# A layer on one core: two of four weight sums by accumulating loads, and a fourth unit with seven products

## The chip, the cores and the metric

The kernel runs on one core of a Trainium2 chip. The metric is the device time of one execution in microseconds (us). The engines are PE (matrix multiply), DVE (vector), ACT (scalar), POOL and SP; SP and ACT issue plain loads, and POOL can issue loads that add what they bring to what stands in the destination.

## The reference

One decoder layer of width 2048 on 256 rows in float32: a SwiGLU half step, two token mixers with gates, and a second SwiGLU half step, each between two RMS norms. The change touches the SwiGLU steps.

```python
def swiglu(x, w_gate, w_up, w_down):                 # 256x2048; 2048x5504 twice; 5504x2048
    return (jax.nn.silu(x @ w_gate) * (x @ w_up)) @ w_down

f1 = swiglu(rms_norm(h, ffn1_pre_norm[l]), ffn1_w_gate[l], ffn1_w_up[l], ffn1_w_down[l])
h = h + 0.5 * rms_norm(f1, ffn1_post_norm[l])
m = hybrid_token_mixer(rms_norm(h, mix_pre_norm[l]), ...)
h = h + rms_norm(m, mix_post_norm[l])
f2 = swiglu(rms_norm(h, ffn2_pre_norm[l]), ffn2_w_gate[l], ffn2_w_up[l], ffn2_w_down[l])
h = h + 0.5 * rms_norm(f2, ffn2_post_norm[l])
```

## The kernel before

A float32 product is made of three matmuls of a cheaper format (`mm3`, L141 to L144): each operand is split into a high part, rounded by ACT (L137), and a low part, the rest, by DVE (L138). `x`, transposed, lies in two row tiles (t = 0, 1) of 128 rows and 16 tiles of 128 along the width; its parts stay in SBUF. Weights come from memory in chunks of two 128-row blocks by up to 512 columns, each split after its load. `raw`, `whi` and `wlo` (chunk, high part, low part) are rings of five buffers.

`ffn` walks over the 5504 columns of gate and up in blocks of 512 (the last has 384). The first block goes through `gemm_block`; the other ten of each ffn go through `gemm_pair`, which makes gate and up of both row tiles at once, in four accumulators `c[t][i]`. It walks over eight units `u` of two weight blocks each. A plain unit takes 2 row tiles x 2 blocks x 2 matrices = 8 products. A unit named in `SUMS` takes seven by Strassen's scheme (Winograd's form): some products take sums of the four weight blocks with sums of the four blocks of `x`, and three products go straight into `c`. Four more accumulators, p1, p5, p6 and p7, gather over the units of `SUMS`, and in the last unit are added to `c` (L260 to L264 and the end of the function). `SUMS` is (2, 4, 6). The sums of `x` (`d`, `s2`, `s3`, `s4`) are made once in each ffn by `operand_sums`.

In a unit of seven products, `ra` holds the two blocks of gate and `rb` those of up. DVE makes the four weight sums with four adds (`wsum` twice, one in place in each of `rb` and `ra`, L248). Split are `ra` and `rb` as chunks, the two sums in `wsum` (into two tiles `wsumh`) and the sum of all four (into the tile `wall`).

The tiles `wsum`, `wsumh`, `wall` and the later `psum` come from a pool `rows` of four buffers of 2 x 512 columns. In `out_proj` the same pool holds eight rows of 512 for the norms, two in a tile.

The engines each run their instructions in order. A tile framework traces the loops, gives a pool's buffers out again when their last reader is done, puts semaphores in, and moves instructions of one engine past each other by its own estimates; so the built order, not the loops, tells what stands behind what. Loads of weights are all on SP's queue: a load that waits for a buffer holds up those behind it.

Of the kernel before, what the change touches and what calls it, by code (L numbers as in the profile page):

```python
# [7 lines left out]
F32 = mybir.dt.float32  # L8
F32R = mybir.dt.float32r
# [3 lines left out]
ALU = mybir.AluOpType  # L13
AX = mybir.AxisListType

P = 128
# [6 lines left out]
CB = 512  # L23
# [4 lines left out]
RW = -(-2 * (16 + CB) * 4 // LINE) * LINE // 4  # L28
STEPS = ((3, 2, 2, 2), (6, 2, 2, 2))
RING = 5  # L30
AHEAD = 3
SUMS = (2, 4, 6)
O_GQ, O_GK, O_GV, O_GO, O_CODE = 0, 512, 1024, 2048, 3072
O_HQ, O_HF, O_HI, O_HO, O_ZG, O_ZH = 3088, 4112, 5136, 6160, 7184, 9232

# [40 lines left out]
def kernel(ctx: ExitStack, tc: tile.TileContext, a: dict, out: bass.AP):  # L76
    nc = tc.nc
# [11 lines left out]
    uid, last = [0], [None]  # L89

    def nm(s):
        uid[0] += 1
        return f"{s}_{uid[0]}"
# [42 lines left out]
    def split_into(hi, lo, src):  # L136
        last[0] = nc.scalar.activation(hi, src, AF.Copy)  # L137
        nc.vector.tensor_tensor(lo, src, hi.bitcast(F32), op=ALU.subtract)  # L138
# [50 lines left out]
    def operand_sums(x, new_part, out):  # L189


        yield
        sl = [slice(2 * SUMS[0] + i, None, 2 * (SUMS[1] - SUMS[0])) for i in range(2)]
        n = len(SUMS)

        def views(s, m):
            t = row_tile(s).rearrange("p i c -> p (i c)")
            return [t[:, i * n * P:(i + 1) * n * P].rearrange("p (k c) -> p k c", c=P)
                    for i in range(m)]

        ab = []
        for t in range(NT):
            ab.append(views("ab", 2))
            for i in range(2):
                nc.vector.tensor_tensor(ab[t][i], x[0][t][:, sl[i], :].bitcast(F32),
                                        x[1][t][:, sl[i], :].bitcast(F32), op=ALU.add)
            yield
        (a11, a12), (a21, a22) = ab
        (d, s2), (s4, s3) = views("sums", 2), views("sums", 2)
# [12 lines left out]
    def gemm_pair(ws, c0, w, lhs, sums, ready):  # L222

        c = [[ps_tile(f"c{t}{i}") for i in range(2)] for t in range(NT)]
        p = {}
        begun = set()
        nu = KT // 2  # L230

        def part(name, u):
            hi, lo = sums[name]
            i = SUMS.index(u)
            return hi[:, i, :], lo[:, i, :]

        def product(ps, x, wp, key, stop=False):
            mm3(ps[:, :w], x, wp, key not in begun, stop)
            begun.add(key)

        def load(i, k0, c0=c0, w=w):
            return wload(ws[i][k0 * P:(k0 + 2) * P, c0:c0 + w].rearrange("(k p) c -> p k c", p=P), w)

        def split(i, k0, c0=c0, w=w):
            return wchunk(None, w, raw=load(i, k0, c0, w))

        def add(o, x, y, op=ALU.add):
            nc.vector.tensor_tensor(o, x, y, op=op)  # L248

        for u in range(nu):  # L250
            k0 = 2 * u
            last_sum = u == SUMS[-1]
            if u not in SUMS:
                if u or not ready:
                    ready = [split(0, k0)] + ([split(1, k0)] if u == nu - 1 else [])
                if u == nu - 1:
                    p1, p5, p6, p7 = [p[s][:, :w] for s in ("p1", "p5", "p6", "p7")]
                    t0, t1 = row_tile("psum"), row_tile("psum")
                    r00, r01, r10, r11 = [t[:, i, :w] for t in (t0, t1) for i in range(2)]
                    nc.scalar.copy(r00, p1)  # L260
# [24 lines left out]
            split_into(allp[:, 0, :], allp[:, 1, :], ra[:, 1, :])  # L285
            if not p:
                for name in ("p1", "p5", "p7", "p6"):
# [22 lines left out]
    def load_bcast(ts, name, n, after):  # L310

        if n % 2 == 0:
            pair = row_tile("row")
            ts += [pair[:, 0, :], pair[:, 1, :]]
        with tc.issue_after(after.ins):
            nc.scalar.dma_start(ts[n], a[name][:, n * CB:(n + 1) * CB].broadcast_to([P, CB]))

    def rstd(ss, n, width, tag):

# [94 lines left out]
    def out_proj(w_dram, nkt, lhs, post, scale, pre, homes, following):  # L414
# [2 lines left out]


        acc = [[None] * 4 for _ in range(NT)]
        wpost, wpre = [], []  # L420
# [13 lines left out]
        for i, (kt, hf) in enumerate(order):  # L434
            parts = load(kt, hf)
            if 6 <= i < 14:

                row, name = (wpost, post) if i < 10 else (wpre, pre)
                if name is not None:
                    load_bcast(row, name, i % 4 + 2 & 3, last[0])  # L440
# [494 lines left out]
    x, rs = new_xT(), [None, None]  # L935
# [34 lines left out]
    def first_of(w_dram, c0):  # L970
        def chunk(i):
# [55 lines left out]
```

## Time and profile before

| | |
|---|---|
| median of 3 runs | 2142.64 us (2141.93 to 2143.45) |
| the profiled execution | 2143.8 us, its span 2142.0 us |
| PE busy | 2130.2 us, 99% |
| DVE, ACT, POOL busy | 1506.8 us (70%), 1101.6 us (51%), 34.6 us (2%) |
| moved | 410.28 MB, 192 GB/s over the span |
| issued by SP as column chunks of gate and up | 512 KB each, 384 KB in the narrow blocks |

A row of the timeline has the start in us, the duration in us, the engine, the line, the operation, the tile written and those read, the shape and the count. A row of groups has line, engine, operation, tiles, shapes and count, then busy us and mean ns of one, then idle us before them with what ended it. A row of waits has engine, line, what was waited for, us in total, times, longest. A row of windows has for each stretch its length, then busy us (and instructions) of PE, of the weight loads, of DVE, ACT and POOL, then PE's clock, the share of the DMA engines and GB/s. A row of DMA issues ends with KB of each and the median us from issue to landing. Matmuls overlap in the pipeline, so what one costs is the distance between starts.

### The profile page before, as it was taken

The page shows a single profiled execution, that of the slowest core. Times are in us where ns is not written, and L with a number is a line of the kernel's source. Part 1 is how long each engine was busy: PE and PEld are TensorE (multiplying, and loading weights), DVE is VectorE, ACT ScalarE, POOL GpSimd, SP SyncE. Part 2 cuts the span into 40 slices and gives each one's busy share as a digit, 9 for nine tenths or more (in the row PEclk, how much of TensorE's full clock was granted, in tenths as well). Part 3 has the DMA queues.
Part 4 walks back from the last instruction along what each step waited for, and adds up shares of the span by engine and source line. Part 5 has one row for each costly group of instructions (what it writes and reads, how often), then busy time and mean ns, then how long its engine had stood idle before and what let it go on. Part 6 is the DMA issues. An engine that isn't in the chain of part 4 may idle for free.

```text
span 2142.0 us, 27066 instructions
## 1 busy us (share of the span) xinstructions
PE 2130.2 (99%) x10024; PEld 1781.7 (83%) x10024; DVE 1506.8 (70%) x1821; ACT 1101.6 (51%) x1375; POOL 34.6 (2%) x87
## 2 busy tenths in 40 slices
PE   9999999999999999999999999999999999999998
PEld 7888888898888888888888888888888888898887
DVE  6889899885455754657575556577889998975455
ACT  7555565554445564444434444465555655554443
POOL 0000000000000100000000000010000000000000
PEclk9999999999999999999999999999999999999999
DMA  7666656667567456555556676755666666576663
GB/s 258 185 198 202 207 179 207 197 201 238 192 194 236 138 177 188 166 158 144 158 160 175 198 207 189 227 195 170 201 201 194 197 197 209 163 247 195 191 194 128
DMA packets 189366, 410.28 MB, mean 192 GB/s; under 512 B 13697, under 2 KB 22305, under 8 KB 189234
## 3 DMA queue, kind: packets, MB, share of 16 engines
q1 hardware_dynamic: 183440, 399.69, 60.8%
q10 hardware_dynamic: 5794, 8.87, 1.3%
q8 instruction: 78, 1.28, 0.2%
q14 instruction: 54, 0.44, 0.1%
HBM read 406.41 MB, written 2.10 MB: 191 GB/s over the span
## 4 chain that ended last, share of the span: by engine, by line
PE 98%; DMA 1%; DVE 1%; ACT 0%; issue 0%; DVEq 0%; POOLq 0%; POOL 0%; ACTq 0%
PE mm L142 10%; PE mm L144 10%; PE mm L143 10%; PE c L143 10%; PE c L142 10%; PE c L144 10%; PE acc L142 9%; PE acc L143 9%; PE acc L144 9%; PE p L144 2%; PE p L143 2%; PE p L142 2%; PE ps L328 2%; PE ps L700 1%; DMA raw<-in_ffn_w_up_dram 0%; PE ps L750 0%
## 5 line engine op out<-in xcount | busy, mean ns | idle before, releaser
L138 DVE TENSOR_TENSOR wlo<-raw,whi 128x1024 fp32r<-128x1024 f32 (+3 forms) x740 | 892.8, 1211 | 524.0 <-ACT whi L137 509.7
L137 ACT ACTIVATE whi<-raw 128x1024 fp32r<-128x1024 f32 (+3 forms) x740 | 777.4, 1051 | 891.9 <-PE mm L143 321.2
L142 PE MATMUL c<-whi,xhi 128*128 128x512 f32 (+1 forms) x860 | 333.0, 387 | 0.0
L144 PE MATMUL c<-wlo,xhi 128*128 128x512 f32 (+1 forms) x860 | 330.1, 384 | 0.0
L143 PE MATMUL c<-whi,xlo 128*128 128x512 f32 (+1 forms) x860 | 330.0, 384 | 0.0
L142 PE MATMUL mm<-whi,xhi 128*128 128x512 f32 (+1 forms) x840 | 326.4, 389 | 1.3 <-ACT xhi L387 1.2
L143 PE MATMUL mm<-whi,xlo 128*128 128x512 f32 (+1 forms) x840 | 321.0, 383 | 0.0
L144 PE MATMUL mm<-wlo,xhi 128*128 128x512 f32 (+1 forms) x840 | 321.0, 383 | 0.0
L142 PE MATMUL acc<-whi,hkhi 128*128 128x512 f32 x640 | 249.2, 389 | 0.0
L144 PE MATMUL acc<-wlo,hkhi 128*128 128x512 f32 x640 | 249.0, 389 | 0.0
L143 PE MATMUL acc<-whi,hklo 128*128 128x512 f32 x640 | 249.0, 389 | 0.0
L144 PEld LDWEIGHTS c<-wlo,xhi 128*128 128x128 f32 x860 | 161.4, 188 | 30.1
L143 PEld LDWEIGHTS c<-whi,xlo 128*128 128x128 f32 x860 | 161.5, 188 | 29.8
L142 PEld LDWEIGHTS c<-whi,xhi 128*128 128x128 f32 x860 | 161.5, 188 | 29.1
L142 PEld LDWEIGHTS mm<-whi,xhi 128*128 128x128 f32 x840 | 158.2, 188 | 31.9 <-ACT xhi L387 2.5
L144 PEld LDWEIGHTS mm<-wlo,xhi 128*128 128x128 f32 x840 | 158.0, 188 | 30.5
L143 PEld LDWEIGHTS mm<-whi,xlo 128*128 128x128 f32 x840 | 158.1, 188 | 29.5 <-issue 0.2
L144 PEld LDWEIGHTS acc<-wlo,hkhi 128*128 128x128 f32 x640 | 120.1, 188 | 25.1
L142 PEld LDWEIGHTS acc<-whi,hkhi 128*128 128x128 f32 x640 | 120.2, 188 | 24.8
L143 PEld LDWEIGHTS acc<-whi,hklo 128*128 128x128 f32 x640 | 120.2, 188 | 24.6
L248 DVE TENSOR_TENSOR wsum<-raw 128x512 f32<-128x512 f32 (+1 forms) x120 | 81.0, 675 | 16.0 <-DMA raw<-in_ffn_w_up_dram 15.0
L138 DVE TENSOR_TENSOR wsumh<-wsum,wsumh 128x1024 fp32r<-128x1024 f32 (+1 forms) x60 | 71.5, 1192 | 0.0
(246 smaller groups left out, 2350.9 us busy)
## 6 DMA issues: line engine op xcount, KB each, us to landing
raw<-in_ffn_w_down_dram SPq DMA_DIRECT2D x172, 512.0 KB, 4.6
raw<-in_w_in_dram SPq DMA_DIRECT2D x168, 512.0 KB, 3.8
raw<-in_ffn_w_up_dram SPq DMA_DIRECT2D x160, 512.0 KB, 3.8
raw<-in_ffn_w_gate_dram SPq DMA_DIRECT2D x159, 512.0 KB, 4.6
raw<-in_w_out_dram SPq DMA_DIRECT2D x32, 512.0 KB, 4.6
raw<-in_w_branch_gla_dram SPq DMA_DIRECT2D x16, 512.0 KB, 3.8
raw<-in_w_branch_hgrn_dram SPq DMA_DIRECT2D x16, 512.0 KB, 4.2
raw<-in_ffn_w_gate_dram SPq DMA_DIRECT2D x16, 384.0 KB, 4.0
```

The costliest lines, as they stand in the source:

```text
L137: last[0] = nc.scalar.activation(hi, src, AF.Copy)
L138: nc.vector.tensor_tensor(lo, src, hi.bitcast(F32), op=ALU.subtract)
L142: nc.tensor.matmul(ps, lhsT=xhi, rhs=whi, start=start, stop=False)
L143: nc.tensor.matmul(ps, lhsT=xlo, rhs=whi, start=False, stop=False)
L144: nc.tensor.matmul(ps, lhsT=xhi, rhs=wlo, start=False, stop=stop)
L248: nc.vector.tensor_tensor(o, x, y, op=op)
L328: nc.tensor.transpose(dst_ps[:, i * P:(i + 1) * P], src[:, i * P:(i + 1) * P], ident)
L700: nc.tensor.matmul(ps[:, i * 64:(i + 1) * 64], lhsT=kT[:, sl], rhs=halves(qT[:, sl])[1], start=True, stop=True)
```

## The change

`SUMS` becomes (1, 3, 4, 6): four units of each block have seven products, and two of them stand next to each other. The blocks of a unit are loaded one by one. `ra` now holds gate's first block and up's second; `rb` holds a sum and gate's second. The two sums of two blocks are made by loads: SP loads up's first block into both halves of `wsum`, and POOL issues for each half a load that adds gate's first or up's second block. DVE makes the two sums of three and four blocks with two adds. `wsum` has three sums side by side and is split into `hi` and `lo` as one, so `wall` is gone. The order of the products changes with the operands. The `rows` pool has three buffers of 3 x 512 columns in place of four of 2 x 512; `psum`, the sums of `x` and the norm rows are laid out for three to a tile, and the last two adds of `psum` become one of twice the width. Other lines are moved in number only.

```diff
-SUMS = (2, 4, 6)
+SUMS = (1, 3, 4, 6)
...
-    rows = ctx.enter_context(tc.tile_pool(name="rows", bufs=4))
+    rows = ctx.enter_context(tc.tile_pool(name="rows", bufs=3))
...
+        def block(i, kt):
+            return ws[i][kt * P:(kt + 1) * P, c0:c0 + w]
...
                     nc.scalar.copy(r00, p1)
-                    add(r01, r00, p6)
-                    add(r10, r01, p7)
-                    add(r01, r01, p5)
-                    add(r11, r10, p5)
+                    add(ru, r00, p6)
+                    add(r10, ru, p7)
+                    add(t1[:, 0:2, :w], t0[:, 1:3, :w],
+                        p5.unsqueeze(1).broadcast_to([P, 2, w]))
...
-            (ra, _), (rb, _) = load(0, k0), load(1, k0)
+            ra, rb = [ring.tile([P, RW], F32, tag="raw", name=nm("raw"))[:, :2 * w]
+                      .rearrange("p (i c) -> p i c", i=2) for _ in range(2)]
+            wsum, hi, lo = [row_tile(n, d)[:, :, :w] for n, d in
+                            (("wsum", F32), ("wsumh", F32R), ("wsuml", F32R))]
+
+            nc.sync.dma_start(ra[:, 0, :], block(0, k0))
+            nc.sync.dma_start(ra[:, 1, :], block(1, k0 + 1))
+            for i in range(2):
+                nc.sync.dma_start(wsum[:, i, :], block(1, k0))
+                nc.gpsimd.dma_start(wsum[:, i, :], block(i, k0 + i), accum_op=ALU.add)
+            nc.sync.dma_start(rb[:, 1, :], block(0, k0 + 1))
             first = wchunk(None, w, raw=(ra, False))
-
-            wsum = row_tile("wsum")[:, :, :w]
-            add(wsum[:, 0, :], rb[:, 1, :], rb[:, 0, :])
-            add(rb[:, 0, :], rb[:, 0, :], ra[:, 0, :])
-            add(wsum[:, 1, :], rb[:, 0, :], rb[:, 1, :])
+            add(rb[:, 0, :], wsum[:, 0, :], ra[:, 1, :])
+            add(wsum[:, 2, :], rb[:, 0, :], rb[:, 1, :])
             second = wchunk(None, w, raw=(rb, False))
-            hi, lo = [row_tile("wsumh", F32R)[:, :, :w] for _ in range(2)]
-            add(ra[:, 1, :], ra[:, 1, :], wsum[:, 1, :])
             split_into(hi, lo, wsum)
-            allp = row_tile("wall", F32R)[:, :, :w]
-            split_into(allp[:, 0, :], allp[:, 1, :], ra[:, 1, :])
+            third = [(hi[:, i, :], lo[:, i, :]) for i in range(3)]
...
             product(p["p1"], lhs(0, k0), first[0], "p1", last_sum)
-            product(c[0][0], lhs(0, k0 + 1), first[1], (0, 0))
-            product(c[0][1], part("s4", u), second[1], (0, 1))
+            product(c[0][1], part("s4", u), first[1], (0, 1))
+            product(c[0][0], lhs(0, k0 + 1), second[1], (0, 0))
             side.pump()
-            product(p["p5"], part("d", u), second[0], "p5", last_sum)
-            product(p["p7"], part("s3", u), (hi[:, 0, :], lo[:, 0, :]), "p7", last_sum)
-            product(p["p6"], part("s2", u), (hi[:, 1, :], lo[:, 1, :]), "p6", last_sum)
-            product(c[1][0], lhs(1, k0 + 1), (allp[:, 0, :], allp[:, 1, :]), (1, 0))
+            product(p["p6"], part("s2", u), second[0], "p6", last_sum)
+            product(p["p5"], part("d", u), third[0], "p5", last_sum)
+            product(p["p7"], part("s3", u), third[1], "p7", last_sum)
+            product(c[1][0], lhs(1, k0 + 1), third[2], (1, 0))
...
     def row_tile(s, dt=F32):
-        return rows.tile([P, 2, CB], dt, tag="row", name=nm(s))
+        return rows.tile([P, 3, CB], dt, tag="row", name=nm(s))
```

What the build makes of it on SP and DVE stands in the prediction, at the places where it is used.

More of the change, by code (lines that the diff above doesn't have):

```diff
@@ L192, in operand_sums, with view @@
         yield
-        sl = [slice(2 * SUMS[0] + i, None, 2 * (SUMS[1] - SUMS[0])) for i in range(2)]
         n = len(SUMS)
[L196 to L199, printed above, removed]
+        groups = [(slice(2 * u0, 2 * u1 + 1, 2 * (u1 - u0)), slice(g, g + 2))
+                  for g, (u0, u1) in zip(range(0, n, 2), zip(SUMS[::2], SUMS[1::2]))]
+        free = []
+        def view():
+            if not free:
+                t = row_tile("sums")
+                free.extend(t[:, i, :n * P].rearrange("p (k c) -> p k c", c=P) for i in range(3))
+            return free.pop(0)
         ab = []
         for t in range(NT):
-            ab.append(views("ab", 2))
             for i in range(2):
[L205 to L209, printed above, removed]
+                ab.append(view())
+                for k, g in groups:
+                    k = slice(k.start + i, k.stop + i, k.step)
+                    nc.vector.tensor_tensor(ab[-1][:, g, :], x[0][t][:, k, :].bitcast(F32),
+                                            x[1][t][:, k, :].bitcast(F32), op=ALU.add)
+                yield
+        a11, a12, a21, a22 = ab
+        d, s2, s3, s4 = [view() for _ in range(4)]
         nc.vector.tensor_tensor(d, a22, a21, op=ALU.subtract)
@@ L258, in gemm_pair @@
                     t0, t1 = row_tile("psum"), row_tile("psum")
-                    r00, r01, r10, r11 = [t[:, i, :w] for t in (t0, t1) for i in range(2)]
+                    r00, ru, r10 = [t0[:, i, :w] for i in range(3)]
+                    r01, r11 = [t1[:, i, :w] for i in range(2)]
                     nc.scalar.copy(r00, p1)
-                    add(r01, r00, p6)
-                    add(r10, r01, p7)
-                    add(r01, r01, p5)
-                    add(r11, r10, p5)
+                    add(ru, r00, p6)
+                    add(r10, ru, p7)
+                    add(t1[:, 0:2, :w], t0[:, 1:3, :w],
+                        p5.unsqueeze(1).broadcast_to([P, 2, w]))
                 for i in range(2):
@@ L280, in gemm_pair @@
+            add(wsum[:, 2, :], rb[:, 0, :], rb[:, 1, :])
             second = wchunk(None, w, raw=(rb, False))
-            hi, lo = [row_tile("wsumh", F32R)[:, :, :w] for _ in range(2)]
-            add(ra[:, 1, :], ra[:, 1, :], wsum[:, 1, :])
             split_into(hi, lo, wsum)
-            allp = row_tile("wall", F32R)[:, :, :w]
-            split_into(allp[:, 0, :], allp[:, 1, :], ra[:, 1, :])
+            third = [(hi[:, i, :], lo[:, i, :]) for i in range(3)]
             if not p:
-                for name in ("p1", "p5", "p7", "p6"):
+                for name in ("p1", "p6", "p5", "p7"):
@@ L307, in row_tile, with load_bcast @@
     def row_tile(s, dt=F32):
-        return rows.tile([P, 2, CB], dt, tag="row", name=nm(s))
[L310 to L314, printed above, removed]
+        return rows.tile([P, 3, CB], dt, tag="row", name=nm(s))
+    def load_bcast(t, name, n, after):
         with tc.issue_after(after.ins):
-            nc.scalar.dma_start(ts[n], a[name][:, n * CB:(n + 1) * CB].broadcast_to([P, CB]))
+            nc.scalar.dma_start(t, a[name][:, n * CB:(n + 1) * CB].broadcast_to([P, CB]))
     def rstd(ss, n, width, tag):
@@ L419, in out_proj @@
         acc = [[None] * 4 for _ in range(NT)]
-        wpost, wpre = [], []
+        wpost, wpre, free = [], [], []
         nxt, rs, ready = ([None] * NT, [None] * NT, [0] * NT), [None, None], []
@@ L439, in out_proj @@
                 if name is not None:
-                    load_bcast(row, name, i % 4 + 2 & 3, last[0])
+                    if not free:
+                        t3 = row_tile("row")
+                        free += [t3[:, j, :] for j in range(3)]
+                    row.append(free.pop(0))
+                    load_bcast(row[-1], name, i % 4 + 2 & 3, last[0])
             for t in range(NT):
```

## The prediction

> **What bounds the kernel now.** I read the head of the page first, then the chain of waits, then what the matrix engine waited for, then one block of columns by its timeline.
>
> ```profile
> span 2142.0 us, 27066 instructions
> PE 2130.2 (99%) x10024; PEld 1781.7 (83%) x10024; DVE 1506.8 (70%) x1821; ACT 1101.6 (51%) x1375; POOL 34.6 (2%) x87
> ...
> PE 98%; DMA 1%; DVE 1%; ACT 0%; issue 0%; DVEq 0%; POOLq 0%; POOL 0%; ACTq 0%
> ...
> PE ps L963 <- POOL idle L960: 1.3, 1, 1.3
> PE mm L142 <- ACT xhi L387: 1.2, 1, 1.2
> PE ps L965 <- DMA wrow<-in_ffn_pre_norm_dram: 0.7, 1, 0.7
> PE ps L328 <- DVE hn L522: 0.7, 2, 0.4
> ...
> SPq L119 <- DVE wlo L138: 1611.1, 662, 16.7
> ```
>
> PE is busy for 99% of the span, and its four groups of waits come to 3.9 us in the whole run. So every matmul taken away is worth its start-to-start time, as long as nothing new makes PE wait. That second half is what this forecast turns on. The stage that changes is the block of columns in `gemm_pair`:
>
> ```profile
> 204.57 0.39 PE L142 MATMUL c<-whi,xhi 128*128 128x512 f32 x1
> ...
> 206.84 0.39 PE L143 MATMUL c<-whi,xlo 128*128 128x512 f32 x1
> ...
> 218.48 0.57 ACT L260 COPY psum<-p 128x512 f32<-128x512 f32 x1
> 430.96 0.59 ACT L260 COPY psum<-p 128x512 f32<-128x512 f32 x1
> 466.15 0.46 ACT L260 COPY psum<-p 128x384 f32<-128x384 f32 x1
> ...
> 176.50:218.50 42.00, 42.00 (x191) 34.84 (x190) 37.76 (x44) 24.05 (x28) 0.00 (x0) 1.00 0.64 200
> ```
>
> The first two rows are ten matmuls apart: 2.27 / 10 = 0.227 us each, so 0.681 us for a product of three. The copy of p1 stands once in each block: (430.96 - 218.48) / 5 = 42.5 us for a block of 512 columns, and 466.15 - 430.96 = 35.2 us for the narrow one of 384. In the window PE is busy for all 42.0 us, DVE for 37.8, ACT for 24.1, and the DMA engines for a share of 0.64 at 200 GB/s. There are 18 wide and 2 narrow blocks (ten in each ffn).
>
> **What the change takes away.** A fourth unit has seven products instead of eight: 0.681 us per wide block, by width 0.51 per narrow one, 18 x 0.681 + 2 x 0.51 = 13.3 us. On DVE a seven-product unit had four adds, three splits of 1024 and one of 512; it has two adds, two splits of 1024 and one of 1536:
>
> ```profile
> L138 DVE TENSOR_TENSOR wlo<-raw,whi 128x1024 fp32r<-128x1024 f32 x698 | 851.4, 1223 | 508.1 <-ACT whi L137 493.7 <-PE ps L328 8.9 <-PE ps L684 1.5
> L137 ACT ACTIVATE whi<-raw 128x1024 fp32r<-128x1024 f32 x698 | 740.4, 1061 | 859.7 <-PE mm L143 318.3 <-PE acc L143 248.0 <-PE c L143 232.8
> L248 DVE TENSOR_TENSOR raw<-raw,wsum 128x512 f32<-128x512 f32 x54 | 37.3, 690 | 1.3
> L138 DVE TENSOR_TENSOR wall<-raw,wall 128x512 fp32r<-128x512 f32 x54 | 37.1, 687 | 0.3 <-ACT wall L137 0.3
> L137 ACT ACTIVATE wall<-raw 128x512 fp32r<-128x512 f32 x54 | 33.3, 617 | 0.0
> L138 DVE TENSOR_TENSOR wlo<-raw,whi 128x768 fp32r<-128x768 f32 x32 | 30.2, 954 | 5.0 <-ACT whi L137 5.0
> L137 ACT ACTIVATE whi<-raw 128x768 fp32r<-128x768 f32 x32 | 27.0, 847 | 26.6 <-PE c L143 21.0 <-ACT wall L137 1.6 <-PE p L143 1.5
> L248 DVE TENSOR_TENSOR raw<-raw,wsum 128x384 f32<-128x384 f32 x6 | 3.3, 556 | 0.1
> L137 ACT ACTIVATE wall<-raw 128x384 fp32r<-128x384 f32 x6 | 3.1, 517 | 0.7 <-DVE raw L248 0.7
> ```
>
> By length, 1536 elements cost DVE 1.22 + (1.22 - 0.69) = 1.75 us and ACT 1.06 + (1.06 - 0.62) = 1.50. DVE's unit falls from 4 x 0.69 + 3 x 1.22 + 0.69 = 7.1 us to 2 x 0.69 + 2 x 1.22 + 1.75 = 5.6; the block as a whole gets about a microsecond lighter, in spite of the fourth unit. DVE was not waited for, so that is worth nothing. Loads grow from 32 column blocks of 256 KB to 44. At the window's share a copy of all 44 would take 0.64 x 42 x 44/32 = 37 us of DMA time, and 44 us if each of the eight accumulating loads counts twice; both stay under the period found below, so bandwidth is not the bound. SP issues 28 loads in place of 16; at 0.37 us (rows below) that is 4.4 us more on a queue that waited 1611 us of the span for raw buffers.
>
> **What the change adds: a loop through one buffer.** The `rows` pool has three buffers and a seven-product unit takes all three: `wsum`, its high part, its low part. `wsum` of a unit is loaded into the buffer which the unit before gives back, and that happens when DVE has split it (of the first unit of a block: when PE has read the last low part of the block before). The build shows it, SP before and now, then DVE now (row names carry the tile's number; in brackets the semaphores that a row waits for):
>
> ```order
> L119 DMA raw_1560<-in_ffn_w_gate_dram 128x2x512
> L119 DMA raw_1562<-in_ffn_w_up_dram 128x2x512
> L119 DMA raw_1605<-in_ffn_w_gate_dram 128x2x512
> L119 DMA raw_1611<-in_ffn_w_up_dram 128x2x512
> L119 DMA raw_1648<-in_ffn_w_gate_dram 128x2x512
> ```
>
> ```order
> L119 DMA raw_1807<-in_ffn_w_up_dram 128x2x512 [waits DMAHW7_49,DMAHW5_49,DVE_49]
> L291 DMA wsum_1742<-in_ffn_w_up_dram 128x512 [waits DMASW7_49,DMASW6_49,PE_49]
> L291 DMA wsum_1742<-in_ffn_w_up_dram 128x512
> ...
> L291 DMA wsum_1827<-in_ffn_w_up_dram 128x512 [waits DMASW1_49,DMAHW5_49,DMASW0_49,DVE_49]
> L291 DMA wsum_1827<-in_ffn_w_up_dram 128x512 [waits DMAHW6_49]
> L293 DMA raw_1871<-in_ffn_w_gate_dram 128x512 [waits DMAHW7_49,DVE_49]
> L119 DMA raw_1915<-in_ffn_w_gate_dram 128x2x512 [waits DMAHW0_49,DVE_49]
> ```
>
> The base of unit 1 (`wsum_1742`) waits for PE, that of unit 3 (`wsum_1827`) for DVE. Behind it on SP stand the other loads of the coming units, which wait too.
>
> ```order
> L257 TENSOR_TENSOR raw_1871<-wsum_1872,raw_1870 128x512
> L257 TENSOR_TENSOR wsum_1872<-raw_1871 128x512
> L138 TENSOR_TENSOR wlo_1889<-raw_1871,whi_1888 128x1024
> L138 TENSOR_TENSOR wsuml_1874<-wsum_1872,wsumh_1873 128x1536
> L138 TENSOR_TENSOR wlo_1918<-raw_1915,whi_1917 128x1024
> ```
>
> That is unit 4: add, add, split of the second chunk, split of the sums, then the next unit's. The add needs the accumulated sum; every later DVE row stands behind it, and ACT's split of the second chunk, on which PE's third product waits, needs the add. So from one unit's `wsum` to the next runs a chain in which nothing overlaps: base load, accumulating load, add, ACT's second split, ACT's split of the sums, DVE's split of the sums, next base load. Its loads are priced by these rows:
>
> ```profile
> raw<-in_ffn_w_up_dram SPq DMA_DIRECT2D x160, 512.0 KB, 3.8
> raw<-in_ffn_w_up_dram SPq DMA_DIRECT2D x16, 384.0 KB, 3.5
> bg<-in_b_branch_gates_dram ACTq DMA_DIRECT2D x8, 256.0 KB, 4.1
> row<-in_ffn_post_norm_dram ACTq DMA_DIRECT2D x8, 256.0 KB, 6.0
> out_dram<-h SPq DMA_DIRECT2D x4, 256.0 KB, 2.1
> ...
> 201.42 0.37 SPq L119 DMA_DIRECT2D raw<-in_ffn_w_up_dram  x1
> ...
> 201.91 1.22 DVE L138 TENSOR_TENSOR wlo<-raw,whi 128x1024 fp32r<-128x1024 f32 x1
> 203.04 1.22 DVE L138 TENSOR_TENSOR wsumh<-wsum,wsumh 128x1024 fp32r<-128x1024 f32 x1
> ```
>
> A base of 256 KB lands after 3.2 us (0.3 less per 128 KB). No row shows an accumulating load, nor any load issued from POOL. Its bounds are the quickest and the slowest 256 KB rows, 2.1 (a store) and 6.0 (rows spread over all partitions); less than the store I leave out, since the accumulating load also reads what it adds to and can't be a gain. I take 4.1, the 256 KB load in 2 KB pieces issued from another queue than SP: it is the nearest in size, piece and issue. Then with L for it, and 0.2 for the handoffs (an estimate: the DVE rows show 0.09 of overlap on one engine, so ACT's first split counts 0.96):
>
> 3.2 + L + 0.69 + 0.96 + 1.50 + 1.75 + 0.2 = 8.3 + L = **12.4 us a unit**.
>
> The step from unit 6 to the next block's unit 1 is longer. Its base stands on SP behind the load of unit 2's up chunk, which needs the raw buffer that DVE frees by the split of the coming unit 0. In DVE's order that comes after two splits and an add: 1.13 + 1.13 + 0.60 + 1.22 (start to start, as in the rows just quoted), and 0.4 to issue: 4.5 us. It then lies behind two 512 KB loads, so lands as they do, 3.8: 0.6 more. A block takes 4 x 12.4 + 4.5 + 0.6 = **54.7 us** against PE's own 42.5 - 0.7 = 41.8. So PE waits some 13 us a block: by the distance of the units in PE's work (15 products from 1 to 3, 7 from 3 to 4, 15 from 4 to 6) 2 to 3 us before units 3 and 6, and 12.4 - 4.8 = 7.6 from unit 3 to 4.
>
> The narrow block by its rows (768 for the second chunk, 768 and the step from 384 for the sums, 192 KB a load): 3.05 + 3.95 + 0.55 + 0.75 + 1.19 + 1.35 + 0.2 = 11.0 a unit, 4 x 11.0 + 4.1 = 48.1 against 35.2.
>
> Sum: 18 x (54.7 - 42.5) + 2 x (48.1 - 35.2) = 220 + 26 = +246 us; the saved product is in it. From the profiled execution's 2143.8 us (1.8 around its span, 1.2 above the median) that makes 2390, about **2389** on the median's scale. The rest costs nothing: the longer sums of x (fp32 256 columns eight times for 384 four times) lie beside the first up block, the wider `psum` tiles replace four adds by three, and the eight rows of the norms are the same loads.
>
> [...]
>
> **The rivals.**
>
> *The loop is hidden, so the saved products count: faster, 2130.* For it speaks that PE's order moves the low parts' matmuls back, and that SP ran up to five raw buffers ahead. It needs 4 x (8.3 + L) + 5.1 below 41.8, so L below 0.9 us; the quickest 256 KB row is 2.1. Chance 0.05. A loop that just reaches the old period (L about 1.0) would be no change: 0.03.
>
> *Accumulating loads land like plain ones, 3.2 or less.* The unit is 11.5, the block 51.1, 18 x 8.6 + 2 x 9 = +173: 2316. At 2.1 it would be +85 or so, 2230. Chance of L between 2.1 and 3.2: 0.14.
>
> *The accumulating load is held up at its issue.* POOL must prepare it while DVE is at work for 37.8 of 42 us. If it has to wait out one DVE instruction of up to 1.75 us in each unit, a block takes 7 us more: 18 x 7 + 2 x 5 = 136 on top, 2525; with an L of its own of 6.0 as well the time passes 2600. The page has POOL at 2% with nothing like it, so nothing speaks against it either. Chance of more than 6.0 in all: 0.08. [...]
>
> **How the numbers follow.** The forecast (the loop with L from 3.2 to 6.0) has 0.70: 2316 to 2143.8 + 18 x 19.8 + 2 x 20 = 2540. The range takes part of the quicker landings and ends at the slowest row: 2270 to 2540, leaving out the hidden loop, the quickest landings and the held-up issue, 2 in 10 together. What this kernel can tell from no change is 0.2%, 4 us. Slower: 0.70 + 0.14 + 0.08 = 0.92; same 0.03; faster 0.05.
>
> **What would show it.** The copy of p1 about 54.7 us apart; PE idle some 13 us a block, most of it before the third product of unit 4, put down to ACT's `whi`, ACT's to DVE's `raw`, DVE's to the load of `wsum`; bases of `wsum` on SP 12 to 13 us apart within a block; DVE busy less than 70% of the span. The landing time of the accumulating load is the number that can prove me wrong: below 1 us the loop is hidden, above 6 the time is beyond my range. If PE shows no waits in the blocks, the buffer is not what I read it to be.

## The result, and the profile after

| | before | after |
|---|---|---|
| median of 4 runs | 2143.05 us (2141.93 to 2146.14) | 2534.55 us (2532.79 to 2538.48) |
| ratio, 95% interval | | 1.183 (1.181 to 1.184) |
| span of the profiled execution | 2142.0 us | 2531.0 us |

The change costs 391 us. The head of the page of after, then the largest group of what PE waited for (total us, times, longest us):

```profile
span 2531.0 us, 27551 instructions
PE 2257.7 (89%) x9964; PEld 1823.9 (72%) x9964; DVE 1492.2 (59%) x1689; ACT 1101.7 (44%) x1335; POOL 176.2 (7%) x247
...
PE c L142 <- ACT whi L137: 213.5, 75, 7.4
```

PE, which hardly waited before, now waits for ACT's high parts of weights in front of a product into `c`. No engine is full: DVE fell from 70% to 59% of a longer span. So the time isn't in the work of an engine but in a chain of waits. Its length is read from the copies of p1, one in a block, and from the windows row of the block between two of them (its columns as in the section on the profile before):

```profile
291.35 0.59 ACT L270 COPY psum<-p 128x512 f32<-128x512 f32 x1
354.45 0.59 ACT L270 COPY psum<-p 128x512 f32<-128x512 f32 x1
...
291.40:354.50 63.10, 49.06 (x194) 37.42 (x193) 37.12 (x38) 24.28 (x26) 7.11 (x8) 0.91 0.71 183
```

This block takes 63.1 us, 20.6 more than the 42.5 of before. By the same copies the wide blocks of the run take 62.3 on average (60.2 to 63.1) and the narrow ones 54.0; 18 x 19.8 + 2 x 18.8 = 394 us is the whole loss. The DMA engines are at a share of 0.71, so bandwidth is not full either. The groups of loads by size (their last number is the median us from issue to landing) show what an accumulating load takes, the last two rows, beside a plain one of the same size:

```profile
raw<-in_ffn_w_gate_dram SPq DMA_DIRECT2D x146, 256.0 KB, 2.8
wsum<-in_ffn_w_up_dram SPq DMA_DIRECT2D x144, 256.0 KB, 3.2
...
wsum<-in_ffn_w_gate_dram POOLq DMA_DIRECT2D x72, 256.0 KB, 4.6
wsum<-in_ffn_w_up_dram POOLq DMA_DIRECT2D x72, 256.0 KB, 5.9
```

One unit (the third with sums in this block) by the timelines of SP, POOL, DVE, ACT and PE; in brackets stands how long the engine was idle before and what ended it:

```profile
325.56 0.80 SPq L291 DMA_DIRECT2D wsum<-in_ffn_w_up_dram  x2
...
329.86 0.88 POOL L292 DMA_DIRECT2D wsum<-in_ffn_w_gate_dram  x1 [13.45 <-DMA wsum<-in_ffn_w_up_dram]
330.40 1.23 POOL L292 DMA_DIRECT2D wsum<-in_ffn_w_up_dram  x1
...
334.31 0.69 DVE L257 TENSOR_TENSOR raw<-wsum,raw 128x512 f32<-128x512 f32 x1 [7.64 <-DMA wsum<-in_ffn_w_gate_dram]
335.04 0.69 DVE L257 TENSOR_TENSOR wsum<-raw 128x512 f32<-128x512 f32 x1
336.26 1.22 DVE L138 TENSOR_TENSOR wlo<-raw,whi 128x1024 fp32r<-128x1024 f32 x1 [0.53 <-ACT whi L137]
338.00 1.76 DVE L138 TENSOR_TENSOR wsuml<-wsum,wsumh 128x1536 fp32r<-128x1536 f32 x1 [0.52 <-ACT wsumh L137]
...
335.17 1.06 ACT L137 ACTIVATE whi<-raw 128x1024 fp32r<-128x1024 f32 x1 [10.48 <-DVE raw L257]
336.49 1.49 ACT L137 ACTIVATE wsumh<-wsum 128x1536 fp32r<-128x1536 f32 x1 [0.26 <-DMA wsum<-in_ffn_w_up_dram]
...
336.28 0.79 PE L142 MATMUL c<-whi,xhi 128*128 128x512 f32 x1 [7.43 <-ACT whi L137]
...
339.79 0.80 SPq L291 DMA_DIRECT2D wsum<-in_ffn_w_up_dram  x2
```

Followed from the top: base at 325.56; it lands after 3.7 us in this unit; POOL issues 0.6 later, at 329.86; the accumulated sum is there after 4.45; DVE adds; ACT splits the chunk, for which PE has stood 7.43 us, then the sums, held 0.26 by the second accumulating load; DVE splits the sums until 339.76; and the next base goes out 0.03 later. That is the loop, 14.2 us long, with no slack in it; the bases of units 3, 4 and 6 go out 0.03 us after a split of the sums in all blocks of this run. How long one load took to land stands in the view of its tile, cut to its issue; for the base of this unit:

```profile
DMA to landing us min/median/max: 3.7/3.7/3.7
```

### The profile page after: what moved, and what is told of

It reads as the page before. It is cut to its first block, busy times and chain, and to the rows that moved or that the text cites. A ratio compares the mean times of both kernels' runs of the same rounds, so it can differ in the third digit from the quotient of the medians.

```text
span 2531.0 us, 27551 instructions
## 1 busy us (share of the span) xinstructions
PE 2257.7 (89%) x9964; PEld 1823.9 (72%) x9964; DVE 1492.2 (59%) x1689; ACT 1101.7 (44%) x1335; POOL 176.2 (7%) x247
## 3 DMA queue, kind: packets, MB, share of 16 engines
q0 software_dynamic: 23040, 40.90, 10.7%
## 5 line engine op out<-in xcount | busy, mean ns | idle before, releaser
L137 ACT ACTIVATE whi<-raw 128x1024 fp32r<-128x1024 f32 (+3 forms) x740 | 760.0, 1045 | 1203.3 <-DVE raw L257 531.1
L142 PE MATMUL c<-whi,xhi 128*128 128x512 f32 (+1 forms) x720 | 296.1, 411 | 213.5 <-ACT whi L137 213.5
L142 PEld LDWEIGHTS c<-whi,xhi 128*128 128x128 f32 x720 | 139.5, 194 | 267.8 <-ACT whi L137 244.6
L144 PE MATMUL c<-wlo,xhi 128*128 128x512 f32 (+1 forms) x720 | 293.1, 407 | 18.3 <-DVE wlo L138 17.4
L257 DVE TENSOR_TENSOR raw<-wsum,raw 128x512 f32<-128x512 f32 (+1 forms) x80 | 54.3, 679 | 431.9 <-DMA wsum<-in_ffn_w_gate_dram 428.1
L143 PE MATMUL c<-whi,xlo 128*128 128x512 f32 (+1 forms) x720 | 283.7, 394 | 0.0
L144 PEld LDWEIGHTS c<-wlo,xhi 128*128 128x128 f32 x720 | 140.1, 195 | 69.1 <-DVE wlo L138 44.0
L143 PEld LDWEIGHTS c<-whi,xlo 128*128 128x128 f32 x720 | 139.7, 194 | 22.7
L138 DVE TENSOR_TENSOR wsuml<-wsum,wsumh 128x1536 fp32r<-128x1536 f32 (+1 forms) x80 | 137.5, 1719 | 28.9 <-ACT wsumh L137 27.1
L292 POOL DMA_DIRECT2D wsum<-in_ffn_w_gate_dram x80 | 69.8, 873 | 1109.1 <-DMA wsum<-in_ffn_w_up_dram 555.4
```

The source lines that it names most:

```text
L142: nc.tensor.matmul(ps, lhsT=xhi, rhs=whi, start=start, stop=False)
L143: nc.tensor.matmul(ps, lhsT=xlo, rhs=whi, start=False, stop=False)
L144: nc.tensor.matmul(ps, lhsT=xhi, rhs=wlo, start=False, stop=stop)
L292: nc.gpsimd.dma_start(wsum[:, i, :], block(i, k0 + i), accum_op=ALU.add)
```

## The experiments

Four theories were set against each other. **1**: the chain through the one free `rows` buffer, whatever its links are; **1b**: a second chain behind it, through the raw buffers on SP's queue; **2**: the adding in the load is what is dear; **3**: the fourth unit, beside the third, is the cause without any load. All times are medians of 4 runs or more beside runs of before on the same chip (2143.0 to 2143.8 us).

| run | time us | ratio to before, 95% interval |
|---|---|---|
| four buffers in common | 2467.41 | 1.151 (1.149 to 1.153) |
| two buffers of its own for `wsum` | 2333.54 | 1.089 (1.087 to 1.090) |
| four sums by DVE, no accumulating load | 2190.69 | 1.022 (1.020 to 1.024) |
| POOL loads without adding | 2427.65 | 1.132 (1.130 to 1.134) |
| no second load at all | 2182.12 | 1.018 (1.017 to 1.020) |
| accumulating loads, three units | 2311.52 | 1.079 (1.077 to 1.080) |
| four sums by DVE, three units | 2142.42 | 1.000 (0.999 to 1.001) |
| own buffers, loads ahead, three units | 2210.38 | 1.031 (1.029 to 1.032) |
| one of the four sums by POOL, four units | 2162.55 | 1.009 (1.007 to 1.010) |
| the same, units 1, 2, 4, 6 | 2162.17 | 1.009 (1.007 to 1.010) |
| own buffers, POOL loads without adding | 2262.09 | 1.057 (1.054 to 1.060) |

### A fourth buffer

```diff
-    rows = ctx.enter_context(tc.tile_pool(name="rows", bufs=3))
+    rows = ctx.enter_context(tc.tile_pool(name="rows", bufs=4))
...
-                u = work.tile([P, CB], F32, tag="tmp", name=nm("u"), bufs=3)
+                if not free:
+                    t3 = row_tile("u")
+                    free.extend(t3[:, j, :] for j in range(3))
+                u = free.pop(0)
...
```

> The pool `rows` gets a fourth buffer, paid for by the three temporary rows, which move into it; the loads and the sums stay. Four units of 14.2 us and one step of 4.9 more make the block of 62 us now.
> The loop through the single buffer alone (theory 1): `wsum` no longer takes the buffer that the last split of sums frees, so a base no longer waits for that split, and PE goes back to its own 41.8 us a block: about 2130 us.
> A second loop behind it (theory 1b): a base stands on SP behind raw loads that need the buffer which DVE's split of the second chunk gives back. That split ends at 337.5 us in the unit in which the split of the sums ends at 339.8, so a unit is about 2 us shorter and the block 8: 2535 - 18 x 8 - 2 x 7 = about 2375, at most 2470.
> That accumulating costs in itself (theory 2), or that the fourth unit stands beside the third (theory 3): no change, 2535.

2467 us: 67 less, at the upper edge of what 1b allowed, far from the 2130 of theory 1 alone. SP, DVE and ACT of this run, around one base:

```profile
309.87 0.34 SPq L288 DMA_DIRECT2D raw<-in_ffn_w_gate_dram  x1
310.38 0.81 SPq L291 DMA_DIRECT2D wsum<-in_ffn_w_up_dram  x2
...
321.14 0.38 SPq L119 DMA_DIRECT2D raw<-in_ffn_w_gate_dram  x1
321.69 0.82 SPq L291 DMA_DIRECT2D wsum<-in_ffn_w_up_dram  x2
...
308.62 1.22 DVE L138 TENSOR_TENSOR wlo<-raw,whi 128x1024 fp32r<-128x1024 f32 x1 [0.53 <-ACT whi L137]
310.25 1.76 DVE L138 TENSOR_TENSOR wsuml<-wsum,wsumh 128x1536 fp32r<-128x1536 f32 x1 [0.40 <-ACT wsumh L137]
...
319.89 1.23 DVE L138 TENSOR_TENSOR wlo<-raw,whi 128x1024 fp32r<-128x1024 f32 x1 [0.48 <-ACT whi L137]
```

The base no longer waits for the split of the sums (310.38, while that split runs from 310.25; no base of this run goes out at the end of such a split). But it stands right behind a raw load that goes out when the split of the second chunk ends: 308.62 + 1.22 = 309.84 and 309.87, 319.89 + 1.23 = 321.12 and 321.14. So there are two loops through the same add, and the buffer only removed the longer one. The step between these two bases is 11.3 us, against 14.2 in the unit shown above; the block (59.3 us) gains less, since other steps grew.

### Two buffers of its own

```diff
-    rows = ctx.enter_context(tc.tile_pool(name="rows", bufs=3))
+    rows = ctx.enter_context(tc.tile_pool(name="rows", bufs=2))
...
     def row_tile(s, dt=F32):
-        return rows.tile([P, 3, CB], dt, tag="row", name=nm(s))
+        tag = "row"
+        if s in ("row", "u", "sums", "wrow", "idle"):
+            turn[0] += 1
+            tag = ("row", "wsum")[turn[0] % 2]
+        elif s == "wsum":
+            tag = "wsum"
+        return rows.tile([P, 3, CB], dt, tag=tag, name=nm(s))
...
```

> As much memory as with a fourth buffer, but `wsum` has two buffers of its own, and the high part, the low part and `psum` share the other two. A base now has to wait only for the split of the sums in the unit before the last.
> Theory 1: the loop now spans two units, so PE's waits fall by more than half: 2130 (all gone) to 2300.
> Theory 1b (the base stands behind raw loads on SP): 2375 to 2470, as with four buffers in common.
> Theories 2 and 3: 2535.

2334 us, with the memory of the run before: half of the loss is gone, but the time misses both ranges and lies between them. What PE waits for has changed. The largest group of its waits, then SP, DVE, ACT and PE in one block:

```profile
PE p L144 <- DVE wsuml L138: 138.4, 20, 8.9
...
286.30 0.80 SPq L291 DMA_DIRECT2D wsum<-in_ffn_w_up_dram  x2
...
301.16 0.82 SPq L291 DMA_DIRECT2D wsum<-in_ffn_w_up_dram  x2
...
284.52 1.75 DVE L138 TENSOR_TENSOR wsuml<-wsum,wsumh 128x1536 fp32r<-128x1536 f32 x1
...
297.04 0.69 DVE L257 TENSOR_TENSOR raw<-wsum,raw 128x512 f32<-128x512 f32 x1 [7.36 <-DMA wsum<-in_ffn_w_gate_dram]
...
299.38 1.75 DVE L138 TENSOR_TENSOR wsuml<-wsum,wsumh 128x1536 fp32r<-128x1536 f32 x1
...
290.46 1.49 ACT L137 ACTIVATE wsumh<-wsum 128x1536 fp32r<-128x1536 f32 x1 [0.93 <-PE c L143]
...
301.19 0.79 PE L144 MATMUL p<-wsuml,hkhi 128*128 128x512 f32 x1 [7.37 <-DVE wsuml L138]
```

138 of the 190 us that are left are one wait in each block, for the low parts of one unit's sums. ACT has made their high parts by 290.46 + 1.49 = 291.95, and DVE's split could follow. It starts at 299.38 only, because in DVE's order it now stands behind the add of the next unit with sums, and that add waits 7.36 us for its own accumulating load. When the split ends, at 301.13, the next base goes out, 0.03 later; the base before it went out at 286.30, 0.03 after the split that ends at 286.27. Of the 80 bases of this run 76 go out like that. So it is still the loop through the buffers of `wsum` that sets the bases, and not the raw loads on SP. The second buffer gives less than the unit of lead that theory 1 counted on, because in units 3 and 4 of each block the split that frees it waits for the next unit's data; in after no split stands behind a later unit's add.

The accumulating loads also landed later than those of after, and the DMA engines were busier; the group of loads and the windows row of one block:

```profile
wsum<-in_ffn_w_gate_dram POOLq DMA_DIRECT2D x72, 256.0 KB, 6.1
...
263.70:314.70 51.00, 43.63 (x189) 35.71 (x188) 36.53 (x38) 25.43 (x25) 6.13 (x8) 0.93 0.85 228
```

A share of 0.85 where after had 0.71, and 6.1 us where it had 4.6.

### The sums by DVE

```diff
-            for i in range(2):
-                nc.sync.dma_start(wsum[:, i, :], block(1, k0))
-                nc.gpsimd.dma_start(wsum[:, i, :], block(i, k0 + i), accum_op=ALU.add)
+            nc.sync.dma_start(rb[:, 0, :], block(1, k0))
             nc.sync.dma_start(rb[:, 1, :], block(0, k0 + 1))
             first = wchunk(None, w, raw=(ra, False))
+            add(wsum[:, 0, :], rb[:, 0, :], ra[:, 0, :])
+            add(wsum[:, 1, :], rb[:, 0, :], ra[:, 1, :])
```

> The fourth unit and the three buffers stay, but there are no accumulating loads: the four blocks come by plain loads into `ra` and `rb`, and DVE makes all four sums with four adds.
> Theory 1: without base and accumulating load (4.3 + 4.5 us a unit) no loop is left that is longer than PE's work. DVE gets two adds more a unit, 8 x 0.69 = 5.5 us a block; it was busy for 37.1 us, so 42.6, just above PE's 41.8. So 2143 + 18 x 0.1 = about 2145, and up to 2190 with handoffs that PE has to wait for.
> Theory 3 (the fourth unit, right behind the third, makes the splits of two units wait for each other): PE still waits several us a block, over 2250.

2191 us, at the edge of theory 1's range: without the loads 344 of the 391 us are gone. Theory 3 falls, since the units stand as they stood. What is left has another cause. The windows row of one block of this run:

```profile
179.10:224.00 44.90, 43.14 (x189) 34.01 (x189) 41.96 (x46) 24.30 (x26) 0.00 (x0) 1.00 0.61 188
```

DVE is busy for 42.0 of 44.9 us, more than PE's own 41.8, and the gaps between its instructions come on top. (PE's 43.1 in the row is not more work, since it makes no more products; what the other 1.3 us are was not shown.)

### POOL loads without adding

```diff
-                nc.gpsimd.dma_start(wsum[:, i, :], block(i, k0 + i), accum_op=ALU.add)
+                nc.gpsimd.dma_start(wsum[:, i, :], block(i, k0 + i))
```

> POOL's loads bring their block without adding it (the additions of gate's first and up's second block are left out); the waits, the order and the bytes read from memory are the same.
> Theory 1 (the chain of waits, whatever the load does): POOL's plain load lands about as late, 4.1 to 4.6 us, and the time stays within 40 us of 2535.
> Theory 2 (the adding in the load is what is dear): it lands like SP's 256 KB, 3.2 us, so 1.4 us a unit are saved, 18 x 4 x 1.4 + 2 x 5 = 110: about 2425.

2428 us, within 3 us of theory 2's number. Groups of loads, POOL's issues and its DMA queue (packets, MB, share of the 16 engines' span) of this run:

```profile
wsum<-in_ffn_w_gate_dram POOLq DMA_DIRECT2D x72, 256.0 KB, 3.4
...
L292 POOL DMA_DIRECT2D wsum<-in_ffn_w_gate_dram x80 | 43.6, 545 | 1057.1 <-DMA wsum<-in_ffn_w_up_dram 575.6 <-DVE hn L537 159.9 <-DVE wlo L138 114.7
...
q0 software_dynamic: 12544, 40.90, 5.3%
```

and the same rows of after:

```profile
L292 POOL DMA_DIRECT2D wsum<-in_ffn_w_gate_dram x80 | 69.8, 873 | 1109.1 <-DMA wsum<-in_ffn_w_up_dram 555.4 <-DVE hn L537 183.9 <-DVE wlo L138 161.0
...
q0 software_dynamic: 23040, 40.90, 10.7%
```

So the adding does have a price: the landing is 1.2 us later (4.6 against 3.4), POOL's issue takes 0.87 us in place of 0.55, and the same 40.9 MB take nearly twice the packets and twice the time of the DMA engines. Per unit that is about 107 / 80 = 1.3 us. But theory 2 as the whole cause falls: 284 us of loss stay when nothing is added.

### No second load

```diff
-                nc.gpsimd.dma_start(wsum[:, i, :], block(i, k0 + i), accum_op=ALU.add)
```

> The eight accumulating loads of a block are left out altogether (so the two sums lack their second block); the bases, the buffers and DVE's and ACT's work stay.
> Theory 1 (the loop through the buffer): a unit of it is shorter by the accumulating load and POOL's handoff, 14.2 - 4.5 - 1.1 = 8.6 us, the block 4 x 8.6 + 4.9 = 39.3, under PE's own 41.8: 2130 to 2170.
> Theory 3 (two units with sums beside each other make their splits wait): over 2250, since units, splits and order are as they were.

2182 us, 12 above theory 1's range and far under theory 3's. The bases still went through the one buffer. The first adds of the units with sums stand at 236.05, 244.98, 254.23, 264.24 and, in the next block, 280.96: 44.9 us where the expectation had 39.3. Of these 5.6 us 3.2 are in the last step: in the windows row that covers nearly all of it DVE is busy for 15.5 of 16.2 us, the adds of `psum` into `c` among it. So there DVE is the limit, and no load. The other 2.4 are in the steps before, where two of the adds still wait for the base (2.75 and 1.71 us).

```profile
264.24:280.45 16.21, 15.65 (x71) 12.62 (x69) 15.49 (x18) 9.04 (x10) 0.00 (x0) 1.00 0.73 231
```

### Three units

```diff
-SUMS = (1, 3, 4, 6)
+SUMS = (2, 4, 6)
```

With the accumulating loads (the sums of `x` are laid out for three):

> The accumulating loads and the three buffers stay; `SUMS` is (2, 4, 6) as before the change: three units with sums, none next to another.
> Theory 1: the loop turns three times a block. Two of its steps take 14.2 us against 15 products (10.2 us) of PE's, so 2 x 4.0 = 8 us a block on top of 42.5; the long step from unit 6 has 22 us of PE's work to hide in. 18 x 8 + 2 x 7 = +158: about 2300, up to 2350 if the long step shows too.
> Theory 3 (the two neighbouring units are the cause): about the time before, 2143.
> A price for each accumulating load, wherever it stands: three quarters of the loss stays, 2436.

2312 us, 12 above theory 1's number. Not the neighbours but the loop against the distance of the units makes the loss, which fell by 57% where a price for each load would take a quarter off.

With DVE's sums in place of the loads (both edits together):

> No accumulating load, four adds on DVE and `SUMS` (2, 4, 6) as before the change; what is left of it is the layout of the buffers, the loads of single blocks and the one wide split of the sums.
> With DVE's adds and the fourth unit 2191 was measured, with DVE busy for over 90% of the blocks. Theory 1 and a full DVE as the cause of those 2191: DVE gets one unit less, about 1.5 us a block, and the time is that before, 2143, within 10 us. If the layout or the wide split costs something of itself: up to 2191.

2142.4 us, no change from before in either direction. The three wide buffers, the loads of single blocks and the one split of 1536 cost and gain nothing.

With two buffers of its own for `wsum` and its two loads written one unit with sums ahead:

```diff
...
+        def fetch(u, c0=c0, w=w):
+            wsum = row_tile("wsum")[:, :, :w]
+            for i in range(2):
+                nc.sync.dma_start(wsum[:, i, :], ws[1][2 * u * P:(2 * u + 1) * P, c0:c0 + w])
+                nc.gpsimd.dma_start(wsum[:, i, :], ws[i][(2 * u + i) * P:(2 * u + i + 1) * P,
+                                                         c0:c0 + w], accum_op=ALU.add)
+            fetched.append(wsum)
...
+            if u != SUMS[-1]:
+                fetch(SUMS[SUMS.index(u) + 1])
...
```

> Two buffers of its own for `wsum`, its loads written one unit with sums ahead, and `SUMS` (2, 4, 6): accumulating loads without the fourth unit. The same two buffers with four units took 2334.
> Theory 1: the loop, 14.2 us long, now spans two units with 15 products between neighbours, 20 us of PE's work; all is hidden: 2143 to 2160.
> A price for each accumulating load by its number or traffic: over 2250.

2210 us, a miss by 50. What DVE waited for in this run:

```profile
DVE raw L267 <- DMA raw<-in_ffn_w_up_dram: 111.4, 31, 5.9
DVE raw L267 <- DMA wsum<-in_ffn_w_gate_dram: 38.7, 11, 7.2
```

The sums are now there in time for most units, but plain loads of up are late in their place. Over a block the DMA engines have a share of 0.81, at 234 GB/s, which looks like room. It is not there where the late loads are: one that SP sends at 282.40 ends DVE's wait at 290.77, and the windows row around it has the DMA engines full:

```profile
278.00:292.00 14.00, 14.00 (x64) 11.59 (x63) 7.28 (x7) 4.72 (x5) 3.50 (x4) 1.00 1.03 315
```

Loads that SP sends beside it land after 7.4 to 8.3 us. In the 8 us before each of the add's waits of over 2.5 us the share is 0.83 to 1.08. PE itself waits at the end of the blocks, 47.8 us in 20 waits, for the `hn` that DVE makes after such an add. So in these stretches the traffic is the limit; whether another order on SP would spread it was not tried.

### One sum on POOL

```diff
             add(wsum[:, 0, :], rb[:, 0, :], ra[:, 0, :])
-            add(wsum[:, 1, :], rb[:, 0, :], ra[:, 1, :])
             add(rb[:, 0, :], wsum[:, 0, :], ra[:, 1, :])
+            nc.gpsimd.tensor_tensor(wsum[:, 1, :], rb[:, 0, :], ra[:, 0, :], op=ALU.subtract)
             add(wsum[:, 2, :], rb[:, 0, :], rb[:, 1, :])
```

> No accumulating loads, four units, as in the run that took 2191; but one of the four adds of a unit goes from DVE to POOL, which had nothing to do in the blocks (the sum of up's first and second block is made there as the sum of three less gate's first).
> Theory 1, with a full DVE (41.5 of 44.4 us a block) as the cause of the rest: DVE loses four adds, started 0.6 us apart, 2.4 us a block, and the block falls by as much, to PE's own 41.8 or 42.5: 2130 to 2148.
> The rest came from the place of the fourth unit and the handoffs there: 2191 stays.
> POOL's add holds DVE up, or is slow enough that the split of the sums waits for it: more than 2191.

2163 us: 28 of the 47 us came back, so DVE's load was a good part of that rest; but it is 15 above the range. POOL and DVE of one unit:

```profile
239.22 1.75 POOL L295 TENSOR_TENSOR wsum<-raw,raw 128x512 f32<-128x512 f32 x1 [8.76 <-DVE raw L257]
...
240.35 1.70 DVE L138 TENSOR_TENSOR wlo<-raw,whi 128x1024 fp32r<-128x1024 f32 x1 [0.54 <-ACT whi L137]
242.53 1.76 DVE L138 TENSOR_TENSOR wsuml<-wsum,wsumh 128x1536 fp32r<-128x1536 f32 x1 [0.48 <-ACT wsumh L137]
244.20 1.22 DVE L138 TENSOR_TENSOR wlo<-raw,whi 128x1024 fp32r<-128x1024 f32 x1
```

DVE's split that runs beside POOL's subtraction takes 1.70 us, and the same split alone 1.22. In this unit that is most of the 0.6 us that DVE saved by the add. Over the run the 698 splits of that size took 872.2 us in place of 844.7, so 27 of the 43 us of adds that DVE was spared in the wide blocks came back. The time fell by more than the rest, so what else the move did for the chain stays open.

```diff
-SUMS = (1, 3, 4, 6)
+SUMS = (1, 2, 4, 6)
```

> As the run with one add on POOL, with `SUMS` (1, 2, 4, 6): the neighbours are the first two units and no longer the middle ones.
> A full DVE as the cause: the same as with (1, 3, 4, 6), within 8 us, since each engine's work in a block is the same.
> The neighbours' place as the cause: another time by more than that.

2162.2 us, the same: where the neighbours stand doesn't matter once the loads are plain.

### Own buffers without adding

The edits of the second and the fourth experiment together.

> `wsum` with two buffers of its own, which took 2334, and POOL's loads without the adding (the additions of gate's first and up's second block are left out).
> The adding costs by its later landing wherever it stands on the chain: with one buffer it was 2535 - 2428 = 107 us; here, where the accumulating loads landed after 6.1 us and DVE waited 231 us for them, again 100 or more: 2230 or less.
> The remaining loss with two buffers is a matter of SP's order alone: 2334 stays, less 20 at most.

2262 us, 71 less than with the adding, where 100 or more were expected. The same group of loads:

```profile
wsum<-in_ffn_w_gate_dram POOLq DMA_DIRECT2D x72, 256.0 KB, 4.5
```

The landing is 4.5 us in place of 6.1. So the adding costs two thirds of what it cost with the tighter chain (107 us), and neither of the two expectations is right. The 118 us that are still lost are mostly the wait of the run with two buffers and adding, shorter by now:

```profile
PE p L144 <- DVE wsuml L138: 84.6, 20, 6.1
```

Again 76 of the 80 bases go out 0.03 us after a split of the sums that stands behind the next unit's add in two units of each block.

## Why the prediction was right, and where it was short

The forecast was 2389, the time is 2535, inside the range of 2270 to 2540 but at its end. By its steps:

- **What bounds the kernel now**: right. PE was full before (99% of the span); after, it waits (89%).
- **What the change takes away**: 13.3 us of products, and a lighter DVE, which was said to be worth nothing. DVE's work in a block is 37.1 us after and 37.8 before. Where DVE does the four sums, the kernel with four units is slower than that with three (2191 against 2142), and still slower with one sum on POOL (2163); in no run did the fourth unit pay.
- **A loop through one buffer**: the mechanism was right, link by link, and its buffer was the one named; taking it away moved the time. What the prediction did not see is how little one more buffer helps: a second loop stands right behind it on SP (the fourth buffer gave back 67 of 391 us), and with two buffers for `wsum` the loop still turns once a unit in half of the units.
- **The chain of a unit, 12.4 us, and the long step, 17.5**: mis-sized, in one half of the chain. The four units of a block by the starts of the base on SP, of POOL's issue and of DVE's add, and the next base:

| unit | base | POOL's issue | add | next base |
|---|---|---|---|---|
| 1 | 295.77 | 301.78 | 306.08 | 311.47 |
| 3 | 311.47 | 314.63 | 320.45 | 325.56 |
| 4 | 325.56 | 329.86 | 334.31 | 339.79 |
| 6 | 339.79 | 343.40 | 349.27 | 358.88 |

```profile
295.77 0.88 SPq L291 DMA_DIRECT2D wsum<-in_ffn_w_up_dram  x2
...
301.78 0.88 POOL L292 DMA_DIRECT2D wsum<-in_ffn_w_gate_dram  x1 [19.09 <-DMA wsum<-in_ffn_w_up_dram]
...
306.08 0.69 DVE L257 TENSOR_TENSOR raw<-wsum,raw 128x512 f32<-128x512 f32 x1 [3.11 <-DMA wsum<-in_ffn_w_gate_dram]
...
358.88 0.88 SPq L291 DMA_DIRECT2D wsum<-in_ffn_w_up_dram  x2
```

  From the add to the next base the four steps take 5.4, 5.1, 5.5 and 9.6 us, where the prediction had three times 5.1 and 9.6: that half, with ACT's and DVE's splits and the order on SP, was right to 0.7 us a block. From the base to POOL's issue they take 6.0 + 3.2 + 4.3 + 3.6 = 17.1 us, where "base load 3.2" and 0.6 for the two 512 KB loads ahead made 13.4. From POOL's issue to the add they take 4.3 + 5.8 + 4.5 + 5.9 = 20.4, where L = 4.1 made 16.4. So the terms that failed are before the add, 3.7 and 4.0 us a block. Of the 3.7, four times 0.56 or 2.2 is POOL's time from the landing of the base to its issue, for which no term stood (the sum had 0.2 for all handoffs of a unit); 1.5 is the landing of the bases. The 4.0 is the accumulating load, 4.3 to 5.9 where 4.1 was taken. This block is among the longest. On average a wide one takes 62.3 - 54.7 = 7.6 us more than forecast and a narrow one 54.0 - 48.1 = 5.9: 18 x 7.6 + 2 x 5.9 = 149 us, where the forecast was short by 146.
- **PE's waits**: 63.1 - 49.1 = 14.0 us a block (13 said), 7.4 of it from unit 3 to 4 (7.6 said). That the sum of the waits came out so near is luck: the block is 8.4 us longer than forecast, and PE's busy time, 49.1 us in place of 42, took up most of that. One part of it is the clock, which over the block was granted at 0.91, and late in the wait of 7.43 us and after it at 0.50:

```profile
334.00:340.00 6.00, 3.72 (x9) 2.95 (x10) 4.61 (x5) 4.57 (x5) 0.00 (x0) 0.50 0.57 130
```

  The matmul after that wait takes 0.79 us where one took 0.39. PE's busy time in windows of half a microsecond, times the missing share of the clock, comes to about 4.3 us of the block (an estimate); the cause of the rest stays open. As the steps of the loop add up to the whole period, I read the slower clock as hidden behind the loop and not as a cost on top; its own price was not measured.
- **Bandwidth is not the bound**: right for after (share 0.71). But the doubled count for accumulating loads, which the prediction only allowed for, is real: 10.7% of the DMA time for bytes that take 5.3% without adding.
- **The rivals**: the hidden loop and L up to 3.2 fall by the landing of 4.6 and 5.9 us. A load held up at its issue by DVE's work falls too. From the landing of the base to POOL's issue pass 0.56 to 0.61 us in every unit of this run whose landing is on record, 61 of 80, and in 27 of these DVE was at work on an instruction with more than 0.3 us to go, most often a split.

## What to carry to other kernels

Before a load into a buffer is made to wait for another load, count the whole ring: what frees the buffer, what stands ahead of that on the engine that frees it, the queue's order ahead of the load, each landing, and one handoff for each engine that takes part; the period is that sum over the units that the buffers span, however idle every engine is. Two buffers span two units only if the work that frees one does not stand behind the next unit's data; the order as built tells (with two buffers 76 of the 80 bases still went out 0.03 us after a split of the sums). Taking the longest loop away shows the next one (a fourth buffer gave back 67 of 391 us), so an added buffer is priced by the second-longest, not by PE's own work. An adding load is not a free add: here DVE does it in 0.69 us, and the load needed 1.2 us more to land than a plain one (4.6 against 3.4) and twice its DMA time (10.7% against 5.3%).

## What the runs showed of the hardware

- In after the first accumulating load of a unit (256 KB, issued by POOL) landed after 4.6 us in the median, the second after 5.9. Without adding the first landed after 3.4. Their issues took 0.87 and 1.18 us on average with adding and 0.55 without.
- The bytes being the same (40.90 MB), POOL's accumulating loads of after took 23040 packets and 10.7% of the DMA engines' span, the same loads without the adding 12544 and 5.3%.
- Landings of equal loads differed within one block of after: the first base of a unit landed after 5.5, 2.6 and 3.7 us in units 1, 3 and 4, the first accumulating load after 4.3, 5.8, 4.4 and 5.9 in units 1, 3, 4 and 6.
- A subtraction of 128x512 on POOL took 1.64 us on average, 1.75 in the unit shown, and a split of DVE beside it 1.70 in place of 1.22.
- In after POOL issued the accumulating load 0.56 to 0.61 us after the base had landed, in the 61 units on record; in 27 of them DVE had more than 0.3 us of an instruction to go.
- With the DMA engines full for 14 us (share 1.03), plain loads of 256 KB landed after 7.4 to 8.3 us, where the median in after is 2.8 to 3.2.
- In 6 us that begin late in an idle time of PE of 7.43 us and end after it, the granted clock was 0.50; over the block it was 0.91.
